# Four PSUM banks in turn for the mLSTM projections and gate tiles; modulation sums with two accumulators and a later row product

## The chip, the cores and the metric

The kernel runs on one core of a Trainium2 chip. The metric is the device time of one execution in microseconds (us), the median over several runs. TensorE is called PE in the profile (its weight loads PEld), VectorE DVE, ScalarE ACT, GpSimd POOL and SyncE SP; SP mostly issues transfers. PSUM is the memory that PE writes its results to. Here it is used as 8 banks of 128 partitions by 512 floats.

## The reference

One layer of a bidirectional sequence model, on 1024 latent tokens and 256 context tokens of width 1024, all in float32. Modulation is a matrix product of silu(c) with `w_mod`: its first 2048 columns shift and scale the tokens ahead of the mixing, the other 4096 gate and scale what comes later in the layer. Cut to what matters here:

```python
mod = silu(c) @ w_mod + b_mod                  # 6 pieces of 1024
sh1, sc1, g1, sh2, sc2, g2 = split(mod, 6)
p = u @ w_in + b_in                            # u: modulated tokens, latent and context
qk = silu(short_conv(concat([q_m, k_m]), conv_qk))        # 3 taps along the tokens
h_m = bidirectional(mlstm_scan, ...)           # 8 heads of width 128
h_g = bidirectional(gla_scan, ...)             # 4 heads, keys 128 wide, values 256
y_m = (head_norm(h_m) * sigmoid(o_m)) @ w_branch_mlstm
y_g = (head_norm(h_g) * silu(z_g)) @ w_branch_gla
mix = (sigmoid(gate_a) * y_m + sigmoid(gate_b) * y_g) @ w_out
h = layer_norm(ALPHA * x + g1 * mix)
out = layer_norm(ALPHA * h + g2 * conv_glu(h * (1 + sc2) + sh2))
```

## The kernel before

The program is written as straight Python over tiles. A framework's list scheduler then puts the instructions of each engine into a fixed order, in which the engine works them off; it also sets the waits between engines. A tile has a tag, and each tag has a number of buffers that its tiles take in turn: a new tile waits until the last reader of the tile that held its buffer before is done. The PSUM tags are `pj`, `pa`, `po` and `pt`, with two banks each.

Every product in float32 is made as three matmuls (`mm3`, L283 to L285): operands are split into a rounded high part and a rest (`whi` and `wlo` for weights, by ACT L252 and DVE L253), and high x high, high x low and low x high are added up in PSUM. The contraction of 1024 takes 8 such triples, so one group of 24 matmuls fills one bank. `proj(w, c, b, tag)` is one group: 128 output channels for block b of the tokens (b 0 and 1: 512 latent tokens each; b 2: the 256 context tokens), into a tile of the given tag, `pj` if none is given.

The stages that the change touches:

- *mLSTM heads* (about 500 to 1120 us). The loop over 8 heads issues the projections and convolution of the next head (`ml_proj_qk`: two groups for q, three for k), for even heads from 2 on the values of two heads (`ml_proj_v`), and the scan of the present head (`ml_scan`), then one or two gate tiles (`fill`, `gate_tile`: two groups each). A group of `ml_proj_qk` is read from PSUM by ACT (L732, the middle tap) and DVE (L727, the two outer taps, L737, the edge column that the next block needs; L743 and L745 correct the ends). A gate tile is read by ACT L537 and stored by an ACT transfer (L538) to `thb` or `tha`. `ml_scan` loads masks and gate rows by POOL transfers (L760, L761 `rr`, L764 `re`), of which ACT makes exponentials (L765, L769). Its PE steps: transposes of k (L777, `pt`), scores q x k (L786, two tiles of `pa`, read by DVE L788), state updates (L796, `pt`), outputs (L816 and L817, `po`). A head's end (L844 on PE, L845 on ACT) is issued one head later. The last GLA head, ahead of this stage, also leaves a `pa` tile that DVE L690 reads.
- *GLA branch with the modulation sums* (about 1195 to 1350 us). Eight output tiles j, each of two groups (24 matmuls), whose PSUM tag goes round `pj`, `pa`, `po` (`ytag`). For each tile SP loads `thb` (L953), ACT makes the tanh, DVE multiplies (L957) and SP stores `ya` (L958). Beside each tile one eighth of the 4096 late modulation columns is worked out: `mod_sum(j)` fills an accumulator with zeros (POOL L901), loads the bias into its first row (SP L903), loads `w_mod` in four pieces of 512 KB into two raw buffers in turn (u16 and u18, SP L906), and adds them up with eight DVE instructions (L908). `mod_row` sums over the 128 partitions by one PE instruction with a vector of ones (L913, into `pt`), which the profile counts as two matmuls; DVE copies the row back (L914) and SP stores it to `md_d` (L915).

The accumulators and raw buffers are tags with one buffer each, u16 to u19, which the gated stages before and after use for other things. The order of a loop body is where the scheduler starts from; it may move instructions past others.

Of the kernel before, what the change touches and what calls it, by code (L numbers as in the profile page):

```python
# [15 lines left out]
P = 128  # L16
# [20 lines left out]
def layer_kernel(ctx, tc, I, out, dbg=None):  # L37
# [39 lines left out]
    def ubt(i, shape, dt=F32):  # L77
        return ub.tile(shape, dt, tag=f"u{i}", name=nm(f"u{i}"))
# [35 lines left out]
    for l in range(7):  # L114
        h = 1 << l
# [207 lines left out]
    def proj(w, c, b, tag="pj"):  # L323
        p = pt(tag, [P, 512])
        mm3(p[:, 0:BW[b]], lambda k: w(k, c, P), u_blk(b))
        return p
# [202 lines left out]
            parts.append((hi, lo))  # L529
        return lambda k, c, n: tuple(t[:, k % 4, c:c + n] for t in parts[k // 4])  # L530

    def gate_tile(dst, off, cb0, j):
        w = wtile(w_in, off + j * P)
        for b in range(2):
            p = proj(w, 0, b)
            t = sc.tile([P, 512], F32, tag="gt", name=nm("gt"), bufs=2)
            A.activation(t[:], p[:], AF.Identity, scale=0.5, bias=cB(cb0 + j))  # L537
            A.dma_start(dst[j][:, b * 512:b * 512 + 512], t[:])  # L538
# [178 lines left out]
    def ml_proj_qk(h):  # L717
        w = wload([(w_in, O_QM + h * P, P, 0), (w_in, O_KM + h * P, P, P)])
        res = []
        for i in range(2):  # L720
            n = SEQ if i == 0 else L
            y = slot((0, 4)[h % 2] + i, [P, n])
            t0, t1, t2 = (cB(c_cv + 16 * j + 8 * i + h) for j in range(3))
            bs, b0, b2 = (cvb[:, j, 8 * i + h:8 * i + h + 1] for j in range(3))

            def tap(o, src, t):
                V.scalar_tensor_tensor(y[:, o:o + src.shape[1]], src, t, y[:, o:o + src.shape[1]],  # L727
                                       op0=ALU.mult, op1=ALU.add)
            for b in range(2 + i):
                m, o = BW[b], b * 512  # L730
                p = proj(w, i * P, b)
                A.activation(y[:, o:o + m], p[:, 0:m], AF.Identity, scale=t1, bias=bs)  # L732
                tap(o + 1, p[:, 0:m - 1], t0)
                tap(o, p[:, 1:m], t2)
                if b == 0:
                    ed = sc.tile([P, 1], F32, tag="ed", name=nm("ed"), bufs=2)
                    V.tensor_copy(ed[:], p[:, m - 1:m])  # L737
                if b == 1:
                    tap(o, ed[:], t0)
                    tap(o - 1, p[:, 0:1], t2)  # L740

                if b != 1:
                    V.tensor_tensor(y[:, o:o + 1], y[:, o:o + 1], b0, op=ALU.subtract)  # L743
                if b != 0:
                    V.tensor_tensor(y[:, o + m - 1:o + m], y[:, o + m - 1:o + m], b2, op=ALU.subtract)  # L745
            th = slot(15, [P, n])
            A.activation(th[:], y[:], AF.Tanh, scale=1.0 / QS if i == 0 else 1.0)
            V.scalar_tensor_tensor(y[:], th[:], 1.0, y[:], op0=ALU.add, op1=ALU.mult)
            res.append(y)
        return res  # L750
# [104 lines left out]

    gates = [(thb_d, O_GB, c_gb, j) for j in range(8)] + [(tha_d, O_GA, c_ga, j) for j in range(8)]

    def fill(n):
        for _ in range(n):
            gate_tile(*gates.pop(0))  # L860

    for h in range(GH):
        q, k = gla_qk(h) if h else (q0, k0)
# [13 lines left out]
    for h in range(MH):  # L877
        nxt = ml_proj_qk(h + 1) if h + 1 < MH else None
        if h and h % 2 == 0:
            v2 = ml_proj_v(h // 2)  # L880
        late()
        rest.append(ml_scan(h, *qk, v2[h % 2]))
        qk = nxt
        fill(2 if h < 2 or h > 5 else 1)
    late()
    while gates:
        fill(1)
# [9 lines left out]
        return tags[seq[0] % 3]  # L897

    def mod_sum(b):
        acc = ubt(19, [P, 512])  # L900
        G.memset(acc[:], 0.0)  # L901
        c0 = 2048 + b * 512
        SY.dma_start(acc[0:1, :], I["b_mod"][c0:c0 + 512].unsqueeze(0))  # L903
        for k2 in range(0, KD, 2):
            raw = ubt((16, 18)[k2 // 2 % 2], [P, 2, 512])
            SY.dma_start(raw[:], I["w_mod"][k2 * P:(k2 + 2) * P, c0:c0 + 512].rearrange("(k p) c -> p k c", p=P))  # L906
            for i in range(2):
                V.scalar_tensor_tensor(acc[:], raw[:, i, :], sC[:, k2 + i, 0:1], acc[:], op0=ALU.mult, op1=ALU.add)  # L908
        return acc

    def mod_row(b, acc):
        p = pt("pt", [P, 512])
        T.matmul(p[0:1, :], ones[:], acc[:], start=True, stop=True)  # L913
        V.tensor_copy(acc[0:1, :], p[0:1, :])  # L914
        SY.dma_start(md_d[b * 512:b * 512 + 512].unsqueeze(0), acc[0:1, :])  # L915

    def gated(off, cb0, src_d, silu):
        hi, lo = [], []
        for j2 in range(4):
            w = wload([(w_in, off + j2 * 256, 256, 0)])  # L920
            for e in range(2):
                j = 2 * j2 + e
                hi.append(slot(j, [P, SEQ], F32R))
                lo.append(slot(8 + j, [P, SEQ], F32R))
                hr = ubt(16 + j % 2, [P, SEQ])
                SY.dma_start(hr[:], src_d[j][:])
                ht = ubt(18, [P, SEQ])
                zz2 = ubt(19, [P, 2, 512]) if silu else None
                for b in range(2):
                    s_ = slice(b * 512, b * 512 + 512)  # L930
                    p = proj(w, e * P, b, ytag())
                    th = sc.tile([P, 512], F32, tag="gt", name=nm("gt"), bufs=2)
                    A.activation(th[:], p[:], AF.Tanh, scale=0.5, bias=cB(cb0 + j))
                    hs = hr[:, s_]
                    if silu:
                        zt = zz2[:, b, :]
                        A.activation(zt, p[:], AF.Identity, scale=0.5, bias=cB(cb0 + j))
                        V.tensor_tensor(hs, zt, hs, op=ALU.mult)
                    V.scalar_tensor_tensor(ht[:, s_], th[:], 1.0, hs, op0=ALU.add, op1=ALU.mult)
                    split(hi[j][:, s_], lo[j][:, s_], ht[:, s_])  # L940
        return hi, lo

    ya_d = [drt(f"ya{j}", [P, SEQ]) for j in range(8)]
    ghi_, glo_ = gated(O_ZG, c_zg, hg_d, True)
    for j2 in range(4):
        w = wload([(I["w_branch_gla"], j2 * 256, 256, 0)])
        for e in range(2):
            j = 2 * j2 + e
            acc = mod_sum(j)
            for b in range(2):  # L950
                s_ = slice(b * 512, b * 512 + 512)
                th = sc.tile([P, 512], F32, tag="gt", name=nm("gt"), bufs=2)
                SY.dma_start(th[:], thb_d[j][:, s_])  # L953
                A.activation(th[:], th[:], AF.Tanh)
                p = pt(ytag(), [P, 512])
                mm3(p[:], lambda k: w(k, e * P, P), lambda k: (ghi_[k][:, s_], glo_[k][:, s_]))
                V.scalar_tensor_tensor(th[:], th[:], 1.0, p[:], op0=ALU.add, op1=ALU.mult)  # L957
                SY.dma_start(ya_d[j][:, s_], th[:])  # L958
            mod_row(j, acc)

    rowF = ubt(19, [P, 3, P])
    cw = [I["ffn_conv_w"][a, b] for a in range(3) for b in range(3)]
# [305 lines left out]
```

## Time and profile before

| | |
|---|---|
| median of three runs | 2344.84 us (2343.28 to 2349.64) |
| profiled execution | 2350.07 us, its span 2348.3 us |
| mean granted PE clock | 0.988 |
| busy: PE, PEld, DVE, ACT, POOL | 96%, 84%, 58%, 31%, 13% |
| DMA over the span | 239.42 MB, mean 102 GB/s |
| chain that ended last | PE 29%, DVE 1%, others under 1% |

The page gives the busy time of each engine; a table by windows gives the same for any stretch of time with the granted clock; the list of waits says for each line of an engine which instruction it waited for last, for how long in all, how often, and the longest. In the timeline a row is a start, a duration, the engine, the line, the operation, output and input tiles; the bracket at its end is the idle time ahead of it and what ended it. Matmuls overlap, so their starts are to be compared, not their durations. A row that ends in x2 or more stands for several instructions in sequence.

### The profile page before, as it was taken

What the parts mean: (1) busy time and instruction counts of PE and PEld (TensorE: products, weight loads), DVE (VectorE), ACT (ScalarE), POOL (GpSimd) and SP (SyncE); (2) the same over time, 40 slices, a digit from 0 to 9 for tenths busy, and PEclk for the clock granted to TensorE, in tenths of its full rate; (3) what the DMA queues carried; (4) which work ended last, traced back from release to release, by engine and by line L of the source; (5) the groups of instructions that cost most, each with busy time, mean ns of one, the idle gap of its engine ahead of it and who ended that gap; (6) DMA issues with size and microseconds to landing.
All of it is one profiled execution on the core that took longest, in us unless ns stands there. A gap on an engine that the chain in (4) does not pass through costs nothing. (4 is left out here: it accounts for less than half of the span.)

```text
span 2348.3 us, 33481 instructions
## 1 busy us (share of the span) xinstructions
PE 2265.5 (96%) x13081; PEld 1965.0 (84%) x13081; DVE 1363.5 (58%) x2695; ACT 719.4 (31%) x1231; POOL 301.1 (13%) x254
## 2 busy tenths in 40 slices
PE   8989999998999999998999999999999999989998
PEld 4979898987889888897877788997888888889998
DVE  6484736475564645655345543577566556567457
ACT  3563323324332322313431143214333333311110
POOL 1010101111110111101210032101110000034300
PEclk9999999999999999999999999999999999999999
DMA  8222121203441333323357544512111122245511
GB/s 280 80 103 75 41 65 46 61 17 105 108 112 53 104 86 99 99 81 110 97 167 232 186 147 139 175 64 81 37 53 54 61 74 72 77 135 186 196 55 64
DMA packets 200848, 239.42 MB, mean 102 GB/s; under 512 B 16801, under 2 KB 155681, under 8 KB 200689
## 3 DMA queue, kind: packets, MB, share of 16 engines
q1 hardware_dynamic: 183521, 188.61, 25.8%
q0 software_dynamic: 8960, 31.63, 5.2%
q10 hardware_dynamic: 8208, 17.04, 2.0%
q8 instruction: 103, 1.69, 0.3%
q14 instruction: 56, 0.46, 0.1%
HBM read 183.42 MB, written 45.41 MB: 97 GB/s over the span
## 5 line engine op out<-in xcount | busy, mean ns | idle before, releaser
L252 ACT ACTIVATE whi<-raw 128x512 fp32r<-128x512 f32 x314 | 197.3, 630 | 516.1 <-PE pj L285 214.5
L283 PE MATMUL pj<-u,whi 128*128 128x512 f32 (+1 forms) x816 | 317.3, 389 | 20.3 <-DVE s L743 8.5
L253 DVE TENSOR_TENSOR wlo<-raw,whi 128x512 fp32r<-128x512 f32 x314 | 229.5, 735 | 157.5 <-ACT whi L252 153.4
L284 PE MATMUL pj<-u,whi 128*128 128x512 f32 (+1 forms) x816 | 314.3, 385 | 0.0
L285 PE MATMUL pj<-u,wlo 128*128 128x512 f32 (+1 forms) x816 | 313.8, 385 | 0.0
L283 PE MATMUL pj<-s,whi 128*128 128x512 f32 x784 | 305.6, 390 | 0.0
L285 PE MATMUL pj<-s,wlo 128*128 128x512 f32 x784 | 305.4, 390 | 0.0
L1120 DVE SCALAR_TENSOR_TENSOR acc<-g,colF,acc 128x945 f32<-128x945 f32 (+2 forms) x168 | 205.0, 1220 | 155.7 <-ACT acc L1111 153.6
L284 PE MATMUL pj<-s,whi 128*128 128x512 f32 x744 | 290.1, 390 | 2.3 <-POOL s L1075 2.3
L283 PE MATMUL pj<-whi,u 128*128 128x256 f32 x768 | 218.0, 284 | 0.0
L285 PE MATMUL pj<-whi,u 128*128 128x256 f32 x768 | 217.6, 283 | 0.0
L284 PE MATMUL pj<-wlo,u 128*128 128x256 f32 x768 | 217.6, 283 | 0.0
L283 PEld LDWEIGHTS pj<-u,whi 128*128 128x128 f32 x816 | 156.1, 191 | 51.2 <-ACT s L769 14.6
L285 PEld LDWEIGHTS pj<-u,wlo 128*128 128x128 f32 x816 | 156.0, 191 | 26.7
L284 PEld LDWEIGHTS pj<-u,whi 128*128 128x128 f32 x816 | 156.3, 192 | 25.9
L283 PEld LDWEIGHTS pj<-s,whi 128*128 128x128 f32 x784 | 147.2, 188 | 30.9
L285 PEld LDWEIGHTS pj<-s,wlo 128*128 128x128 f32 x784 | 147.2, 188 | 30.8
L284 PEld LDWEIGHTS pj<-s,whi 128*128 128x128 f32 x744 | 139.7, 188 | 33.0 <-POOL s L1075 3.6
L283 PEld LDWEIGHTS pj<-whi,u 128*128 128x128 f32 x768 | 147.4, 192 | 0.5
L284 PEld LDWEIGHTS pj<-wlo,u 128*128 128x128 f32 x768 | 147.4, 192 | 0.0
L285 PEld LDWEIGHTS pj<-whi,u 128*128 128x128 f32 x768 | 147.4, 192 | 0.0
L727 DVE SCALAR_TENSOR_TENSOR s<-pj,colB,s 128x511 f32<-128x511 f32 (+2 forms) x96 | 57.5, 613 | 92.2 <-ACT s L732 91.3
(486 smaller groups left out, 4479.8 us busy)
## 6 DMA issues: line engine op xcount, KB each, us to landing
u<-in_w_mod_dram SPq DMA_DIRECT2D x48, 512.0 KB
raw<-in_w_in_dram SPq DMA_DIRECT2D x96, 256.0 KB
raw<-in_w_up_dram SPq DMA_DIRECT2D x176, 128.0 KB
raw<-in_w_in_dram SPq DMA_DIRECT2D x96, 128.0 KB
raw<-in_w_down_dram SPq DMA_DIRECT2D x44, 256.0 KB
s<-rmask POOLq DMA_DIRECT2D x16, 512.0 KB, 5.2
s<-rr POOLq DMA_DIRECT2D x16, 512.0 KB, 7.9
qq<-re POOLq DMA_DIRECT2D x16, 512.0 KB, 6.5
```

The costliest lines, as they stand in the source:

```text
L252: A.activation(hi, src, AF.Copy)
L253: eng.tensor_tensor(lo, src, hi.bitcast(F32), op=ALU.subtract)
L283: T.matmul(p, lh, rh, start=k == 0, stop=False)
L284: T.matmul(p, lh, rl, start=False, stop=False)
L285: T.matmul(p, ll, rh, start=False, stop=k == nk - 1)
L727: V.scalar_tensor_tensor(y[:, o:o + src.shape[1]], src, t, y[:, o:o + src.shape[1]], op0=ALU.mult, op1=ALU.add)
L1120: V.scalar_tensor_tensor(av, g[:, r0 + dy:r1 + dy, c0 + dx:c1 + dx], convw(3 * ky + kx, f), av, op0=ALU.mult, op1=ALU.add)
```

## The change

Three things are changed. In `ml_proj_qk` the five groups of a head go to `pj` and `pa` in turn (q b0 pj, q b1 pa, k b0 pa, k b1 pj, k b2 pa) instead of all to `pj`. Gate tiles in the mLSTM loop put their second group into `pa`; in the GLA loop they stay with `pj`. And the modulation sums use u17 and u19 in turn as accumulator instead of u19 alone, and the row product of sum j is written behind tile j + 1 instead of behind tile j, the last one behind the loop.

```diff
--- before.py
+++ after.py
@@ -529,10 +529,10 @@
             parts.append((hi, lo))
         return lambda k, c, n: tuple(t[:, k % 4, c:c + n] for t in parts[k // 4])
 
-    def gate_tile(dst, off, cb0, j):
+    def gate_tile(dst, off, cb0, j, tags=("pj", "pj")):
         w = wtile(w_in, off + j * P)
         for b in range(2):
-            p = proj(w, 0, b)
+            p = proj(w, 0, b, tags[b])
             t = sc.tile([P, 512], F32, tag="gt", name=nm("gt"), bufs=2)
             A.activation(t[:], p[:], AF.Identity, scale=0.5, bias=cB(cb0 + j))
             A.dma_start(dst[j][:, b * 512:b * 512 + 512], t[:])
@@ -728,7 +728,7 @@
                                        op0=ALU.mult, op1=ALU.add)
             for b in range(2 + i):
                 m, o = BW[b], b * 512
-                p = proj(w, i * P, b)
+                p = proj(w, i * P, b, ("pj", "pa")[(i + b) % 2])
                 A.activation(y[:, o:o + m], p[:, 0:m], AF.Identity, scale=t1, bias=bs)
                 tap(o + 1, p[:, 0:m - 1], t0)
                 tap(o, p[:, 1:m], t2)
@@ -855,9 +855,9 @@
 
     gates = [(thb_d, O_GB, c_gb, j) for j in range(8)] + [(tha_d, O_GA, c_ga, j) for j in range(8)]
 
-    def fill(n):
+    def fill(n, tags=("pj", "pj")):
         for _ in range(n):
-            gate_tile(*gates.pop(0))
+            gate_tile(*gates.pop(0), tags)
 
     for h in range(GH):
         q, k = gla_qk(h) if h else (q0, k0)
@@ -881,7 +881,7 @@
         late()
         rest.append(ml_scan(h, *qk, v2[h % 2]))
         qk = nxt
-        fill(2 if h < 2 or h > 5 else 1)
+        fill(2 if h < 2 or h > 5 else 1, ("pj", "pa"))
     late()
     while gates:
         fill(1)
@@ -897,7 +897,7 @@
         return tags[seq[0] % 3]
 
     def mod_sum(b):
-        acc = ubt(19, [P, 512])
+        acc = ubt((17, 19)[b % 2], [P, 512])
         G.memset(acc[:], 0.0)
         c0 = 2048 + b * 512
         SY.dma_start(acc[0:1, :], I["b_mod"][c0:c0 + 512].unsqueeze(0))
@@ -942,11 +942,12 @@
 
     ya_d = [drt(f"ya{j}", [P, SEQ]) for j in range(8)]
     ghi_, glo_ = gated(O_ZG, c_zg, hg_d, True)
+    accs = {}
     for j2 in range(4):
         w = wload([(I["w_branch_gla"], j2 * 256, 256, 0)])
         for e in range(2):
             j = 2 * j2 + e
-            acc = mod_sum(j)
+            accs[j] = mod_sum(j)
             for b in range(2):
                 s_ = slice(b * 512, b * 512 + 512)
                 th = sc.tile([P, 512], F32, tag="gt", name=nm("gt"), bufs=2)
@@ -956,7 +957,9 @@
                 mm3(p[:], lambda k: w(k, e * P, P), lambda k: (ghi_[k][:, s_], glo_[k][:, s_]))
                 V.scalar_tensor_tensor(th[:], th[:], 1.0, p[:], op0=ALU.add, op1=ALU.mult)
                 SY.dma_start(ya_d[j][:, s_], th[:])
-            mod_row(j, acc)
+            if j:
+                mod_row(j - 1, accs[j - 1])
+    mod_row(7, accs[7])
 
     rowF = ubt(19, [P, 3, P])
     cw = [I["ffn_conv_w"][a, b] for a in range(3) for b in range(3)]
```

Line numbers up to L940 are the same in both programs; in the loop over the GLA tiles they are one higher behind the change (L953 is L954, L957 is L958, L958 is L959).

The first place is ACT's order in one head in the middle of the stage, around the reads of its q and k groups. In these rows `pj_993`, `_995`, `_998` and `_1000` are the groups q b0, q b1, k b0 and k b1, `s0` and `s1` hold q and k, `s6` and `s7` the masks, `qq` the gate rows. Before:

```order
L769 ACTIVATE s6_1008_7006<-s6_1008_7006,ta_4662 128x128 x7
L732 ACTIVATE s0_992_6828<-pj_993_6829,cvb_402,colB_389 128x512
L769 ACTIVATE s6_1008_7006<-s6_1008_7006,ta_4662 128x128
L769 ACTIVATE s7_1010_7021<-s7_1010_7021,ta_4662 128x128 x4
L765 ACTIVATE qq_1006_7004<-qq_1006_7004 128x1024
L769 ACTIVATE s7_1010_7021<-s7_1010_7021,ta_4662 128x128 x4
L732 ACTIVATE s0_992_6828<-pj_995_6860,cvb_402,colB_389 128x512
L747 ACTIVATE s15_996_6891<-s0_992_6828 128x1024
L732 ACTIVATE s1_997_6894<-pj_998_6895,cvb_402,colB_389 128x512
L732 ACTIVATE s1_997_6894<-pj_1000_6926,cvb_402,colB_389 128x512
```

Now:

```order
L769 ACTIVATE s6_1008_7006<-s6_1008_7006,ta_4662 128x128 x8
L732 ACTIVATE s0_992_6828<-pj_993_6829,cvb_402,colB_389 128x512
L769 ACTIVATE s7_1010_7021<-s7_1010_7021,ta_4662 128x128 x4
L765 ACTIVATE qq_1006_7004<-qq_1006_7004 128x1024
L769 ACTIVATE s7_1010_7021<-s7_1010_7021,ta_4662 128x128 x4
L732 ACTIVATE s0_992_6828<-pa_995_6860,cvb_402,colB_389 128x512
L747 ACTIVATE s15_996_6891<-s0_992_6828 128x1024
L732 ACTIVATE s1_997_6894<-pa_998_6895,cvb_402,colB_389 128x512
L732 ACTIVATE s1_997_6894<-pj_1000_6926,cvb_402,colB_389 128x512
```

The groups q b1 and k b0 have moved to `pa`; one exponential (L769) has gone ahead of the first L732, and else ACT's order is the same.

The second place is PE's order around the first row product (L913) of the branch stage. `pa_1511` is the first of the two groups of tile j = 1, `po_1512` in the new program the second, `pj_1532` the first group of tile 2, `u19_1495` and `u17_1495` the accumulator of sum 0. Before:

```order
L283 MATMUL pa_1511_10577<-s5_1444_10214,whi_1490_10462 128x512
L284 MATMUL pa_1511_10577<-s13_1445_10215,whi_1490_10462 128x512
L285 MATMUL pa_1511_10577<-s5_1444_10214,wlo_1491_10463 128x512
L913 MATMUL pt_1504_10551<-u19_1495_10472,ones_77 1x512
L283 MATMUL pa_1511_10577<-s6_1465_10308,whi_1493_10468 128x512
L284 MATMUL pa_1511_10577<-s14_1466_10309,whi_1493_10468 128x512
```

Now:

```order
L285 MATMUL po_1512_10603<-s6_1465_10308,wlo_1494_10469 128x512
L283 MATMUL po_1512_10603<-s7_1474_10378,whi_1493_10468 128x512
L284 MATMUL po_1512_10603<-s15_1475_10379,whi_1493_10468 128x512
L285 MATMUL po_1512_10603<-s7_1474_10378,wlo_1494_10469 128x512
L913 MATMUL pt_1513_10630<-u17_1495_10472,ones_77 1x512
L283 MATMUL pj_1532_10680<-s0_1377_9818,whi_1515_10636 128x512
L284 MATMUL pj_1532_10680<-kk_1378_9819,whi_1515_10636 128x512
```

Before, the first L913 stands behind 18 of the 24 matmuls of a group of tile 1, with 67 to 77 rows from each L913 to the next and the last three behind the start of the next gated stage. Now it stands behind the last matmul of tile 1, and the next six follow at the end of a tile each (49 rows apart); the eighth comes 27 rows into the next gated stage.

The third place is SP's order around the store of the first row (L915) and the bias load (L903) of a later sum. Before:

```order
L906 DMA u18_1507_10562<-in_w_mod_dram 128x2x512
L953 DMA gt_1512_10604<-thb1_867 128x512
L915 DMA md_d_9785<-u19_1495_10472 1x512
L958 DMA ya1_9787<-gt_1510_10574 128x512
L263 DMA raw_1553_10840<-in_w_branch_gla_dram 128x2x256
L903 DMA u19_1505_10555<-in_b_mod_dram 1x512
L953 DMA gt_1532_10681<-thb2_868 128x512
```

Now:

```order
L959 DMA ya1_9787<-gt_1511_10600 128x512
L915 DMA md_d_9785<-u17_1495_10472 1x512
L906 DMA u16_1527_10661<-in_w_mod_dram 128x2x512
L954 DMA gt_1533_10707<-thb2_868 128x512
L903 DMA u17_1526_10658<-in_b_mod_dram 1x512
L906 DMA u18_1528_10665<-in_w_mod_dram 128x2x512
L959 DMA ya2_9788<-gt_1531_10677 128x512
```

Before, the bias load for sum 1 follows the store of row 0, since both use u19. Now the bias loads of sums 0 and 1 stand together ahead of these rows, and behind the store of row 0 comes the bias load of sum 2, with the first piece of `w_mod` for that sum ahead of it.

## The prediction

> **What bounds the kernel now.** I first read the page's busy shares, then a table by stage, then PE's waits in the two stages that the change touches, and last the timeline around single waits.
>
> ```profile
> PE 2265.5 (96%) x13081; PEld 1965.0 (84%) x13081; DVE 1363.5 (58%) x2695; ACT 719.4 (31%) x1231; POOL 301.1 (13%) x254
> ```
>
> PE is busy 96% of a span of 2348.3 us, so only PE's idle time and its slow-clock time can be had: every other engine counts only where it makes PE wait. The profiled execution took 2350.07 us, 5.2 above the median of 2344.84. By stage (stretch and length, then busy time and instructions of PE, PEld, DVE, ACT, POOL, then granted clock, DMA share, GB/s):
>
> ```profile
> 480.00:640.00 160.00, 150.34 (x855) 129.56 (x856) 100.88 (x221) 56.67 (x113) 23.54 (x26) 0.97 0.30 81
> 640.00:840.00 200.00, 194.53 (x1191) 172.09 (x1191) 118.06 (x363) 56.30 (x112) 23.52 (x24) 0.99 0.34 93
> 840.00:1100.00 260.00, 245.38 (x1574) 220.56 (x1573) 141.60 (x436) 76.40 (x162) 33.85 (x29) 0.97 0.34 93
> 1195.00:1365.00 170.00, 161.24 (x664) 123.38 (x663) 89.64 (x129) 38.99 (x64) 15.04 (x17) 0.98 0.64 201
> ```
>
> The mLSTM heads (480 to 1100) leave PE idle for 30 us of 620, the GLA branch with the modulation sums (1195 to 1365) for 9 of 170. PE's waits, from 480 to 1120 and then from 1195 to 1365, with POOL's there (total us, times, longest):
>
> ```profile
> PE pj L283 <- DVE s L743: 8.5, 4, 2.9
> PE pt L777 <- ACT s L845: 6.1, 1, 6.1
> PE pj L283 <- DVE s L727: 5.5, 3, 2.7
> PE pj L283 <- ACT gt L537: 5.2, 2, 2.7
> ```
> ```profile
> PE pt L913 <- DVE u L908: 5.4, 5, 2.1
> PE pt L913 <- issue: 3.3, 2, 1.7
> ```
> ```profile
> POOL u L901 <- DMA md_d<-u: 128.4, 7, 20.0
> ```
>
> The three rows `pj L283` are 19.2 us in nine waits: a projection wants a pj bank that its evacuation has not left. The L777 row waits for an operand, which no bank cures. The L913 rows, 8.7 us in seven waits, are the row product waiting for its sum. One `pj` wait close up, PE first, then ACT, then DVE:
>
> ```profile
> 787.17 0.39 PE L285 MATMUL pj<-u,wlo 128*128 128x512 f32 x1
> 790.42 0.77 PE L283 MATMUL pj<-u,whi 128*128 128x512 f32 x1 [2.86 <-DVE s L743]
> 793.12 0.47 PE L283 MATMUL pj<-u,whi 128*128 128x512 f32 x1
> 793.43 0.39 PE L284 MATMUL pj<-u,whi 128*128 128x512 f32 x1
> 793.65 0.39 PE L285 MATMUL pj<-u,wlo 128*128 128x512 f32 x1
> 785.74 2.16 ACT L769 ACTIVATE s<-s,ta 128x128 f32<-128x128 f32 x7 [2.31 <-DMA s<-rr]
> 787.80 0.76 ACT L732 ACTIVATE s<-pj,cvb,colB 128x512 f32<-128x512 f32 x1
> 788.67 1.53 DVE L727 SCALAR_TENSOR_TENSOR s<-pj,colB,s 128x511 f32<-128x511 f32 x2 [7.72 <-ACT s L732]
> 790.24 0.16 DVE L743 TENSOR_TENSOR s<-s,cvb 128x1 f32<-128x1 f32 x1
> ```
>
> At full clock these matmuls start 0.22 to 0.23 us apart (793.43, 793.65), so a group of 24 is 5.45 us. The last matmul before the wait (787.17) closes the second group, so the first ended at about 781.9. Its evacuation (L732, two L727, the edge columns) ends at 790.4, 8.5 us after the group, because ACT works in order and stood first behind the gate exponentials L769, which had waited for a transfer of `rr`. With two banks the third group needs the bank 5.45 us after the first ended, so 3 us are lost. After the wait the clock is low: from 790.42 to 793.12 there are six steps in 2.70 us, 1.33 more than at full clock, and the next step is 0.31; that is 1.4 us more for such a wait. I count such a slow stretch, by this spacing, after four of the seven waits outside head 0 (636, 790, 930, 991).
>
> By the Trainium skill, page "TensorE: Matmul & The Clock Gate", section "What's actually happening", the clock falls only after an idle window of about 3.4 us. By that rule waits of 2 to 3 us would cost no slow clock, and the gain below would be about 14 us instead of 23.5. The measured spacing after 2.86 us decides against it here.
>
> **The change part by part.** It adds no matmul, no transfer and no evacuation.
>
> *Banks in turn, heads 1 to 7.* Groups go q b0 pj, q b1 pa, k b0 pa, k b1 pj, k b2 pa, and a gate tile takes one of each. A bank now comes back after two groups or more, 10.9 us, against 8.5 us for the late evacuation above: the wait is gone with 2.4 us to spare, and the cover for all of it is ACT's lateness staying under 10.9. Removed: 19.2 less the two waits of head 0 (2.49 and 0.92, rows below) is 15.8 us in seven waits. Each gap exceeds its recorded wait by 0.16 (787.17 to 790.42 is 3.25, less a step of 0.23, against 2.86), 1.1 in all. Four slow stretches are 5.6. Together 22.5; at least 15.8 if only recorded waits return.
>
> *pa is shared with the score matmuls L786.* Their first group holds a pa bank until DVE's L788; the gate tile's second half wants it some 9 us later in the order. If L788 is as late as the 8.5 above, that is no wait. Their second group comes 2.9 us after k b2 in heads 0, 1, 3 and 5, in the bank that k b2 used. That evacuation is seen here, where k b2's last matmul stands just ahead of L844:
>
> ```profile
> 805.62 1.03 PE L844 MATMUL pt<-ident,s 128*128 128x128 f32 x8
> 808.23 0.47 DVE L727 SCALAR_TENSOR_TENSOR s<-pj,colB,s 128x255 f32<-128x255 f32 x1
> ```
>
> It ends at 808.7, some 3 us behind: waits of 0 to 0.8, and I take 0.4, four times, minus 1.6. In heads 2, 4 and 6 a v projection lies between.
>
> *Head 0.* The last GLA head's output holds the second pa bank until L690, behind these groups, so three groups of head 0 share one pa bank.
>
> ```profile
> 547.96 0.77 PE L283 MATMUL pj<-u,whi 128*128 128x512 f32 x1 [2.49 <-DVE s L743]
> 565.14 0.47 PE L283 MATMUL pj<-u,whi 128*128 128x512 f32 x1 [0.92 <-DVE s L727]
> 551.95 1.66 DVE L727 SCALAR_TENSOR_TENSOR s<-pj,colB,s 128x511 f32<-128x511 f32 x3 [4.00 <-ACT s L732]
> 553.65 0.15 DVE L745 TENSOR_TENSOR s<-s,cvb 128x1 f32<-128x1 f32 x1
> ```
>
> The old waits cost 2.49 + 0.92 + 1.4 of slow clock, 4.8. Now k b0 follows q b1 into the same bank. PE arrives at 545.47 (547.96 less 2.49); 16 matmuls of k b1 stand ahead in the new order (3.6 us), so it stops at 549.1 and waits until q b1 is out, 553.7: 4.6 plus 1.4 is 6.0. Net minus 1.2 (plus 1 if ACT gets q b1 sooner, minus 4 if k b2 then waits as well). Heads: 22.5 - 1.6 - 1.2 = 19.7 us, between 14 and 24.
>
> *Two accumulators and the row one tile later.* Today's sums follow one chain; one link of it on PE, SP, POOL and SP:
>
> ```profile
> 1239.49 1.02 PE L913 MATMUL pt<-u,ones 128*1 128x512 f32 x2 [1.60 <-issue]
> 1241.25 0.25 SPq L915 DMA_DIRECT2D md_d<-u  x1
> 1243.48 0.53 POOL L901 MEMSET u<- 128x512 f32 x1 [20.02 <-DMA md_d<-u]
> 1244.03 0.25 SPq L903 DMA_DIRECT2D u<-in_b_mod_dram  x1
> ```
>
> From the row product to the next bias load 4.5 us pass, and the load must land before a sum starts; with two accumulators this runs beside the other sum. What can be saved: 8.7 recorded, 0.16 for each of seven, and two slow stretches of 1.4, one in each window with a clock of 0.91:
>
> ```profile
> 1215.00:1235.00 20.00, 18.27 (x71) 13.71 (x70) 10.79 (x16) 4.31 (x7) 0.53 (x1) 0.91 0.71 227
> 1255.00:1275.00 20.00, 19.56 (x83) 14.84 (x82) 10.40 (x15) 3.03 (x5) 0.53 (x1) 1.00 0.77 244
> 1295.00:1315.00 20.00, 18.08 (x70) 14.01 (x71) 10.11 (x15) 4.37 (x7) 0.53 (x1) 0.91 0.65 198
> ```
>
> In all 12.6 us. What is late next is the sum's own pace T per tile: both raw buffers are loaded twice for each sum, 512 KB a load. SP's issues of three pairs of consecutive rounds:
>
> ```profile
> 1230.83 1.95 SPq L906 DMA_DIRECT2D u<-in_w_mod_dram  x2
> 1236.77 3.03 SPq L906 DMA_DIRECT2D u<-in_w_mod_dram  x2
> 1268.33 1.96 SPq L906 DMA_DIRECT2D u<-in_w_mod_dram  x2
> 1273.91 0.38 SPq L906 DMA_DIRECT2D u<-in_w_mod_dram  x1
> 1287.59 1.95 SPq L906 DMA_DIRECT2D u<-in_w_mod_dram  x2
> 1295.32 1.96 SPq L906 DMA_DIRECT2D u<-in_w_mod_dram  x2
> ```
>
> Rounds of 5.94, 5.58 and 7.73, mean 6.42, so T is 12.8 us (11.2 to 15.5). I take the mean, since the rounds to come meet the same other transfers. What PE allows: its first row product stands 29 rows later in the new order (5508 against 5479), so near 1223.1, where today's, without its wait, would stand at about 1216.5; the eighth stands 321 rows behind it, 314 matmuls of 0.227 and seven row products of 1.02, so at 1301.5 if PE never waits. The first sum is ready at about 1219.3, a microsecond later than today's (a second fill and bias load go ahead of it), the eighth at 1219.3 + 7T = 1308.9. PE loses 7.4 there, plus 1.4 of slow clock: 8.8, and the net is 12.6 - 8.8 = plus 3.8. With T at 11.2 it is plus 12.6, with 15.5 minus 15. Behind a late load on SP's queue stand the th loads and ya stores; their banks are three tags of two, 32 us deep.
>
> Sum: 19.7 + 3.8 = 23.5 us, from 2350.07 to 2326.6 in this execution; against the median, 2321.
>
> **The rivals.**
> *A. The sums fall behind* (T from 14 to 16.2). For it: the round of 7.73, and DMA engines 64% busy in that stage, which a denser program pushes up. Against it: two of three rounds are under 6. At T = 15 the eighth sum is at 1324.3, PE loses 22.8 + 1.4 against 12.6, 11.6 net, so the gain is 8 us: 2337.
> *B, the other side: the second accumulator does not speed the sums.* If they keep today's spacing of 18.9 us (128.4 / 7 between memsets, and the memset's 0.53) while PE wants rows every 11.9, the eighth sum is at 1351.6: a loss of 50.1 + 1.4 - 12.6 = 38.9, so 19 us slower after the banks' gain: 2364. The whole gain is gone from T = 16.2, and a loss shows from 17.2. Against it: 4.5 us and the bias landing of each 18.9 are the chain that goes.
> *C. The evacuation itself is the limit*: ACT's lateness (8.5 here) passes 10.9 when PE runs ahead, so waits only move to pa, as in head 0. Then the banks give 5, and with 4 from the sums 2336. Against it: DVE is 58% busy and ACT 31%, and the transfers that hold ACT are started after PE's own steps.
> *D. The clock.* If going from bank to bank made PE stumble at each group, 40 q and k groups and 24 gate halves at 1.4 us would cost 90 us: about 2411. Against it: the GLA branch already changes banks among pj, pa and po with each group, and its clock is 1.00 in the window from 1255. The Trainium skill, same page, section "A second HAM failure mode: psum-queue depth-cycling", reports such a case for N=512 matmuls; that row does not agree.
> *E. The sums keep up* (T under 11.9): hardly a wait at all, 30 to 36 us gained, 2308 to 2315.
>
> **How the numbers follow.** Chances: forecast 0.60 (banks 18 to 23, T 11.9 to 14: 2312 to 2331), A 0.13, B 0.05, C 0.10, D 0.02, E 0.10. A measurement of this kernel tells 0.3%, 7 us, from no change: same is 2338 to 2352. Faster: 0.60, 0.08 of A, 0.05 of C and all of E, 0.83. Same: 0.05 of A, 0.04 of C, 0.09. Slower: B, D and 0.01 of C, 0.08. The range 2308 to 2337 leaves out B, D, half of C and half of A.
>
> **What would show it.** Right: from 480 to 1080 the `L283` waits on L743, L727 and L537 are gone but for one of 4 to 6 us in head 0; small waits stand at L786; the L777 wait of 6 us stays. In the branch stage the memsets hardly wait for md_d, rounds of w_mod come every 6 to 6.5 us, and PE waits about 7 us at the last two L913. Wrong: `pa` rows waiting on L727 in many heads (C), L913 waits over all tiles and above 20 us (A, B), or a clock under 0.98 without waits (D).

## The result, and the profile after

| | before | after |
|---|---|---|
| median, first comparison | 2344.06 us (2342.15 to 2349.64) | 2324.14 us (2320.30 to 2327.47) |
| ratio | | 0.9911 (0.9887 to 0.9934) |
| median, second comparison | 2345.23 us (2339.88 to 2349.63) | 2323.13 us (2320.71 to 2323.88) |
| ratio | | 0.9906 (0.9891 to 0.9920) |
| profiled execution, its span | 2350.07, 2348.3 us | 2320.30, 2318.5 us |

The change is worth about 20 to 22 us. The pair of profiles lies 29.8 us apart, since that of before is one of the longest runs of its kernel and that of after the shortest of its own; stage times below are therefore compared over several traces. The page's busy row and the table by stage, with the columns as before:

```profile
PE 2254.1 (97%) x13081; PEld 1958.9 (84%) x13081; DVE 1362.8 (59%) x2695; ACT 719.3 (31%) x1231; POOL 300.4 (13%) x254
```
```profile
480.00:640.00 160.00, 152.83 (x887) 133.10 (x886) 101.22 (x225) 56.84 (x114) 24.67 (x27) 0.98 0.30 79
640.00:840.00 200.00, 199.82 (x1223) 177.16 (x1222) 121.70 (x371) 64.60 (x133) 27.99 (x27) 1.00 0.37 101
840.00:1100.00 260.00, 254.19 (x1635) 229.30 (x1634) 148.05 (x465) 74.86 (x154) 29.54 (x27) 0.99 0.34 96
1180.00:1350.00 170.00, 166.17 (x694) 127.59 (x693) 92.16 (x133) 41.98 (x69) 19.78 (x20) 0.99 0.66 213
```

From 640 to 840 PE is now busy for all but 0.2 us, with the clock at 1.00; before it lacked 5.5. All other engines have the same work. PE's waits in the two stages (480 to 1105, then 1085 to 1460; rows under 1 us left out):

```profile
PE pt L777 <- ACT s L845: 5.7, 1, 5.7
PE pt L501 <- DVE ta L502: 3.2, 1, 3.2
PE pa L283 <- DVE s L727: 3.1, 1, 3.1
```
```profile
PE pj L283 <- ACT whi L252: 3.8, 1, 3.8
```

Of the nine bank waits of the q, k and gate groups (19.2 us) one is left, in head 0; a tenth, of 1.1 us on DVE L713 behind a value group of head 0, which the prediction did not count, is gone too. All waits at L913 are gone in this trace, and one new wait for weights stands at the start of the next gated stage. The same place as in the prediction, a head in the middle, rows of PE, ACT and DVE:

```profile
776.16 0.39 PE L285 MATMUL pj<-u,wlo 128*128 128x512 f32 x1
776.39 0.39 PE L283 MATMUL pa<-u,whi 128*128 128x512 f32 x1
781.83 0.39 PE L283 MATMUL pa<-u,whi 128*128 128x512 f32 x1
787.27 0.39 PE L283 MATMUL pj<-u,whi 128*128 128x512 f32 x1
780.36 2.45 ACT L769 ACTIVATE s<-s,ta 128x128 f32<-128x128 f32 x8 [2.73 <-DMA s<-rr]
782.71 0.75 ACT L732 ACTIVATE s<-pj,cvb,colB 128x512 f32<-128x512 f32 x1
783.58 1.53 DVE L727 SCALAR_TENSOR_TENSOR s<-pj,colB,s 128x511 f32<-128x511 f32 x2 [8.30 <-ACT s L732]
785.15 0.16 DVE L743 TENSOR_TENSOR s<-s,cvb 128x1 f32<-128x1 f32 x1
```

ACT still waits for `rr`, and the first group (its last matmul at 776.16) is read out by 785.3, 8.7 us after its end. Nothing has become faster here; but q b1 (776.39), k b0 (781.83) and k b1 (787.27) start 5.44 us apart without a gap; before, the third group waited 2.86 us for the bank of the first, and now q b1 and k b0 go to `pa` and k b1 to the other `pj` bank. The sums, by POOL's fills of the accumulators, PE's row products, the start of the gated stage on PE and the last adds on DVE:

```profile
1208.06 0.53 POOL L901 MEMSET u<- 128x512 f32 x1 [24.81 <-DVE u L908]
1221.11 0.53 POOL L901 MEMSET u<- 128x512 f32 x1 [12.52 <-DMA md_d<-u]
1234.09 0.53 POOL L901 MEMSET u<- 128x512 f32 x1 [12.45 <-DVE u L908]
```
```profile
L913 PE MATMUL pt<-u,ones x16: 590/591/592, 1200.4 to 1287.4; 128*1 128x512 f32 x16
```
```profile
1237.31 1.02 PE L913 MATMUL pt<-u,ones 128*1 128x512 f32 x2
1282.03 0.79 PE L283 MATMUL pj<-u,whi 128*128 128x512 f32 x1 [3.83 <-ACT whi L252]
1282.62 0.63 PE L284 MATMUL pj<-u,whi 128*128 128x512 f32 x1
1284.91 1.54 DVE L908 SCALAR_TENSOR_TENSOR u<-u,sC,u 128x512 f32<-128x512 f32 x2 [0.74 <-DMA u<-in_w_mod_dram]
```

The fills come 13 us apart instead of 18.9. The first sum ends at 1196.2 and the eighth at 1286.45 (1284.91 + 1.54), so one each 12.9 us. PE puts a row product every 12.3 us. It comes 4.2 us after the first sum (1200.4), and as the sums fall behind by 0.6 each, it comes 0.7 after the seventh. It stands half a microsecond behind the eighth only because the wait for weights and the slow steps after it, 5.6 us together, lie ahead of that row: without them it would have been there at 1281.4, 5.1 us too early. These are the loads of `thb` and of the weights on SP, and what ACT made of them:

```profile
1275.90 0.42 SPq L954 DMA_DIRECT2D gt<-thb  x1
1276.37 0.47 SPq L263 DMA_DIRECT2D raw<-in_w_in_dram  x1
1280.60 0.63 ACT L955 ACTIVATE gt<-gt 128x512 f32<-128x512 f32 x1 [5.82 <-DMA gt<-thb]
1281.34 0.63 ACT L252 ACTIVATE whi<-raw 128x512 fp32r<-128x512 f32 x1
```

ACT stood behind the `thb` load for 5.82 us and split the weights (L252) right after; the trace does not show whether the weights had landed before that.

Stage times over several traces: "heads" from the last L672 to the last L844, "branch" from there to the first transpose of `rowF` (L1022, or L1025 behind the longer loop), all taken from the starts on PE; "rest" is what follows to the end of the span. The stretch ahead of the heads, 500 to 504 us in these traces, is left out.

| kernel | heads | branch | rest |
|---|---|---|---|
| before | 613.1 | 374.9 | 859.4 |
| after | 587.3 | 368.2 | 859.5 |
| after, second trace | 588.8 | 370.4 | 861.8 |
| banks alone | 588.4 | 376.4 | 860.5 |
| sums alone | 607.4 | 371.9 | 859.8 |
| two accumulators alone | 608.1 | 376.3 | 861.5 |
| q and k groups alone | 587.1 | 373.7 | 862.5 |
| q and k all on pa | 604.8 | 372.5 | 861.3 |

Heads with the old banks (before, sums alone, two accumulators alone): mean 609.5; with the new ones (the two traces of after, banks alone): 588.2. That is 21.3 us. The branch with the old sums (before, banks alone, the two q/k kernels): mean 374.4; with the new ones (after twice, sums alone): 370.2, that is 4.2 us. The rest is the same within about 3 us, so that a difference of that size in one stage of one trace says little.

### The profile page after: what moved, and what is told of

Its sections match the earlier page's. It is cut to its first block, busy times and chain, and to the rows that moved or that the text cites. A ratio compares the mean times of both kernels' runs of the same rounds, so it can differ in the third digit from the quotient of the medians.

```text
span 2318.5 us, 33477 instructions
## 1 busy us (share of the span) xinstructions
PE 2254.1 (97%) x13081; PEld 1958.9 (84%) x13081; DVE 1362.8 (59%) x2695; ACT 719.3 (31%) x1231; POOL 300.4 (13%) x254
## 3 DMA queue, kind: packets, MB, share of 16 engines
q1 hardware_dynamic: 183521, 188.61, 25.8%
## 5 line engine op out<-in xcount | busy, mean ns | idle before, releaser
L252 ACT ACTIVATE whi<-raw 128x512 fp32r<-128x512 f32 x314 | 196.7, 630 | 467.9 <-PE pj L285 212.0
L283 PE MATMUL pj<-u,whi 128*128 128x512 f32 (+1 forms) x528 | 207.5, 393 | 3.9 <-ACT whi L252 3.8
L285 PE MATMUL pj<-u,wlo 128*128 128x512 f32 (+1 forms) x528 | 206.2, 390 | 0.0
L284 PE MATMUL pj<-u,whi 128*128 128x512 f32 (+1 forms) x528 | 206.0, 390 | 0.0
L283 PE MATMUL pa<-u,whi 128*128 128x512 f32 (+1 forms) x376 | 141.2, 376 | 3.1 <-DVE s L727 3.1
L284 PE MATMUL pa<-u,whi 128*128 128x512 f32 (+1 forms) x376 | 141.1, 375 | 0.0
L285 PE MATMUL pa<-u,wlo 128*128 128x512 f32 (+1 forms) x376 | 140.2, 373 | 0.0
L283 PEld LDWEIGHTS pj<-u,whi 128*128 128x128 f32 x528 | 100.4, 190 | 23.2 <-ACT whi L252 4.3
```

The source lines that it names most:

```text
L252: A.activation(hi, src, AF.Copy)
L283: T.matmul(p, lh, rh, start=k == 0, stop=False)
L284: T.matmul(p, lh, rl, start=False, stop=False)
L285: T.matmul(p, ll, rh, start=False, stop=k == nk - 1)
```

## The experiments

**Both halves, and the whole again.** The whole change, repeated:

> The whole change once more, to size it: one profile of each kernel shows 29.8 us between them, the medians 19.9. My sum gives 23.5 us, a ratio of 0.990. If the profile pair is the better measure, 0.987; if the medians are, 0.9915. In the trace no pj wait of over 1 us between 500 and 1080 but two in head 0 (about 3 us each), and no wait at L913.

0.9906 (0.9891 to 0.9920), 22.1 us between the medians; no pj wait in the heads, waits of 2.7 and 3.2 in head 0, none at L913, and 4.9 us for the weights of the next gated stage. The medians were the better measure, not the pair of profiles. The banks alone (the lines that pass `tags` on are left out):

```diff
-                p = proj(w, i * P, b)
+                p = proj(w, i * P, b, ("pj", "pa")[(i + b) % 2])
-            p = proj(w, 0, b)
+            p = proj(w, 0, b, tags[b])        # gate tiles of the mLSTM loop: pj, pa
```

> Only the banks in turn (q/k groups and gate tiles), sums as before. Theory: the seven pj waits outside head 0 and their slow clock go, 20 to 23 us, ratio 0.990 to 0.9915, and the L913 waits stay at 8 to 10 us. Rival (the bank waits were only covering waits on ACT's late evacuation that come back elsewhere): under 8 us, ratio above 0.9965, with pa waits on L727 or L537 in several heads.

0.9927 (0.9915 to 0.9939), 17.5 us between the medians. That is a little under the theory's range, and more than double the rival's 8. PE's waits in the heads are those of the whole change, and no other `pa` wait stands there; those of the branch are as before:

```profile
PE pt L913 <- DVE u L908: 7.3, 5, 2.8
PE pt L913 <- issue: 3.0, 2, 1.7
```

The sums alone (the lines that keep the accumulators in `accs` are left out):

```diff
-        acc = ubt(19, [P, 512])
+        acc = ubt((17, 19)[b % 2], [P, 512])
-            mod_row(j, acc)
+            if j:
+                mod_row(j - 1, accs[j - 1])
+    mod_row(7, accs[7])
```

> Only the sums (two accumulators, row product a tile later), banks as before. Theory: a sum each 12.9 us against a PE tile of 12.3 us, so the L913 waits of 8.7 us and two slow stretches go but for one wait of about 4 us at the start of the next gated stage: 6 to 9 us, ratio 0.996 to 0.9975; the pj waits stay at 19 us. Rival (sums bound by the two raw buffers as before): 0 to 3 us.

0.9987 (0.9976 to 0.9998), 3.7 us between the medians: nearer to the rival's 0 to 3 than to the 6 to 9 that I expected. The pj waits are there (16.9 us, and 1.2 at L713, where the trace of before has 19.2 and 1.1), and in the branch stand

```profile
PE pt L913 <- DVE u L908: 3.9, 4, 1.5
PE pj L283 <- ACT whi L252: 3.2, 1, 3.2
```

So 7.1 us of waits stand where the trace of before has 8.7: most of what L913 gave back was taken by the weights' wait. The sums' pace here is 13.6 us from the first end (1213.5) to the eighth (1308.6), well under the 18.7 of before, so the raw buffers did not hold them at the old pace as the rival had it; but it is 0.7 above the 12.9 that the theory took, and the lead of 4.9 us that PE leaves the first sum is used up by the fourth. The whole change is near the same edge: with the same sums, the L913 waits are nothing in both of its traces and 1.6 to 2.2 us in four of the five kernels below that keep whole sums and the later row, at a pace of 12.9 to 13.4 us.

**Two accumulators alone**, with the row product behind its own tile (only the first changed line of the diff above):

> Only the two accumulators; the row product is written behind its own tile as before, which puts the first L913 30 rows (7 us) and the last 14 rows (3 us) ahead of its place in the whole change. Theory: the pace of the sums alone sets it, 12.9 us each, so the eighth sum comes some 8 us after PE wants it: L913 waits of 7 to 10 us in total, spread over the tiles, gain 1 to 4 us, ratio 0.9985 to 0.9995. Rival (the second accumulator is all that counts, the later row nothing): as the sums alone, 6 to 9 us.

1.0010 (1.0001 to 1.0019): no gain, against both. The L913 waits are 10.3 us,

```profile
PE pt L913 <- DVE u L908: 7.3, 5, 3.2
PE pt L913 <- issue: 3.0, 1, 3.0
```

just above the 7 to 10 expected and no less than before, although the eighth sum now ends at 1310.7 instead of 1349.5 (34 us earlier if counted from the stage's start, the last L844). The scheduler has also moved the row products ahead on PE, the last by 164 matmuls of PE's order: it has spent in advance what the faster sums gain. With the row a tile later PE comes 4.9 us (the sums alone) or 4.2 us (the whole change) after the first sum instead of waiting for it, and the slower sums live on that lead.

**Q and k groups alone**, gate tiles left on pj, sums as before (only the first line of the first diff):

> The q and k groups in turn on pj and pa, gate tiles all on pj, sums as before. Theory (a bank is late when it comes back after one group, 5.45 us, and its evacuation ends 7 to 9 us after the group): the waits on L743, L727 and L737 go, and those on L537 (5.2 us, two) go too, since k's groups no longer stand in the pj banks ahead of the gate tiles' second use: 17 to 20 us, ratio 0.9915 to 0.993, as the banks with the gates. Rival (each kind of tile needs its own four banks): the two waits on L537 stay, about 7 us with their slow clock, ratio 0.995.

0.9913 (0.9900 to 0.9927), 19.0 us: the gain of the banks is there without the gate tiles. No wait on L537 is left in the heads:

```profile
PE pt L777 <- ACT s L845: 5.9, 1, 5.9
PE pt L501 <- DVE ta L502: 3.2, 1, 3.2
PE pa L283 <- DVE s L727: 1.5, 1, 1.5
PE pt L501 <- ACT whi L252: 0.5, 1, 0.5
PE pa L786 <- DVE s L727: 0.4, 1, 0.4
```

**All q and k groups on pa**, the control for the theory of the distance:

```diff
-                p = proj(w, i * P, b)
+                p = proj(w, i * P, b, "pa")
```

> All q and k groups on pa, gate tiles on pj, sums as before: as many banks in the stage as with the change, but q and k have two in turn. Theory (what counts is the number of groups until a bank comes back): the waits of 2.5 to 3 us return at `pa <- DVE s L743` and `L727`, 12 to 16 us with head 0, and only the two waits on L537 go: gain 4 to 8 us, ratio 0.9965 to 0.998. Rival (q and k were held up by gate and value tiles in the same two banks, and four banks for the stage are enough however they are dealt): 15 to 20 us, ratio 0.992 to 0.9935.

1.0009 (0.9998 to 1.0019): no gain. The waits are back under the other name, 15.2 us, within the 12 to 16 of the theory:

```profile
PE pa L283 <- DVE s L743: 9.8, 5, 3.0
PE pa L283 <- DVE s L727: 4.1, 3, 1.7
PE pa L283 <- ACT s L769: 1.3, 1, 1.3
```

The waits on L537 went, as expected, but the gain of 4 to 8 us did not come. Its heads are 4.7 us shorter than the mean of the old ones in the one trace, which with 2341.07 us was the shortest of its ten runs (median 2348.80). This trace has one slow stretch at a projection outside head 0, where that of before has four, and its mean granted clock is 0.991 against 0.987 to 0.990 in the nine others; more slow stretches there would fit, but no trace shows them. For the rival it is decisive: the stage has the same four banks here, and what counts is how many groups pass until a bank comes back (the releasers L743 and L727 are the evacuation of q and k, not the score tiles that share `pa`).

**Gate tiles left on pj, with the sums:** the change less its gates' part.

> The whole change with the gate tiles left in pj. Theory (the q and k groups in turn remove the gate tiles' waits too, so the gates' own turn is worth nothing): within 2 us of the whole change, ratio to before 0.9895 to 0.9915, and no wait on L537. Rival (the stage times of the q/k version, 587.1 us for the heads against 588.4 with the gates, show that gate tiles in pa cost something at L786): 2 to 4 us below the whole change, ratio 0.989 or less.

0.9889 (0.9872 to 0.9906), 27.8 us between the medians, with the before of this comparison at 2347.84 against 2344.1 to 2345.4 in the others. No wait on L537 came back. Its own median, 2320.03, is 3.1 below the whole change, but the intervals overlap (0.9891 to 0.9920), and its trace, of the longest of its five runs (2325.86), shows no shorter stage (heads 591.0, branch 369.7). By the ratio it lies on the rival's side, but no term of the trace carries that; the runs can't tell the gates' part from nothing.

**Head 0 on po instead of pa:**

```diff
-                p = proj(w, i * P, b, ("pj", "pa")[(i + b) % 2])
+                p = proj(w, i * P, b, ("pj", "pa" if h else "po")[(i + b) % 2])
```

> The whole change, but head 0 takes po instead of pa, whose banks are not held by the last GLA head's late tile. Theory (the remaining wait at k b0 of head 0, 2.5 to 3.1 us in three traces, is a bank held by that tile): it goes with its slow clock, 3 to 4.5 us below the whole change, ratio to before 0.9885 to 0.9895. Rival (ACT's waits for the mask and gate-row transfers in head 0 are what PE waits for): the wait moves to the next use of a bank or to L777 of head 0, 0 to 1 us, ratio 0.9905.

0.9921 (0.9908 to 0.9933), 17.8 us: no better than the whole change. The wait at k b0 has gone, so it was that bank; but the time has not:

```profile
PE pt L692 <- DVE hn L690: 2.5, 1, 2.5
```

PE now waits nearly as long at the transposes of the last GLA head, whose operand DVE L690 makes behind the late taps. The rival is nearer in time and named the wrong place; for its cause speaks that in this trace ACT waits 8.52 us for a mask and 1.64 us for `rr` (L769) among the reads of these groups.

**Half of each sum:** only two of the four `w_mod` pieces are loaded and added.

> The whole change with only the first two of the four w_mod pieces loaded and added per sum: half of each sum is left out. Theory (after the change the wait of 3 to 5 us at the start of the next gated stage, `pj L283 <- ACT whi L252`, comes from SP and the DMA engines being filled with w_mod and the sums only just keep up): sums of 6 to 7 us, no wait at L913, and the whi wait shrinks under 1.5 us: 3 to 6 us below the whole change, ratio 0.988 to 0.9895. Rival (the weights of the gated stage are late because of the order on SP, behind ya stores that follow PE): the wait stays at 3 to 5 us and the time within 2 us of the whole change.

0.9901 (0.9886 to 0.9917), 0.4 us from the whole change between the medians. The wait for weights is gone, but a wait at L913 of almost the same length has come:

```profile
PE pt L913 <- DVE u L908: 4.3, 1, 4.3
```

Two things moved with the shorter sums. The scheduler put the weights' loads for the next gated stage ahead on SP (the third is issued at 1248.81, in the whole change at 1276.37), so this run does not tell whether the filled DMA engines or the order on SP made them late. And it put the eighth row product directly behind the seventh; the eighth sum, whose accumulator comes free only after the sixth row product, is ready at 1278.35 for a PE that is there 4 us before. So neither theory holds for the time: one wait has taken the place of the other, as in the whole change the eighth sum (1286.45) ends 4.4 us after the wait for weights does (1282.03).

**The transposes at a head's end, and half of the gate tables, in po instead of pt:** the first edit alone, the second alone, and both.

```diff
-                p = pt("pt", [P, 4, P])          # L844, finish of ml_scan
+                p = pt("po", [P, 4, P])
-                p = pt("pt", [P, 8, 64])         # L501
+                p = pt("pt" if j0 == 0 else "po", [P, 8, 64])
```

> The whole change, with the two transposed tiles at a head's end (L844) in po instead of pt. The wait of 5.3 to 6.1 us at L777 in the last head is there in every trace; its releaser L845 reads pt. Theory (this too is a bank that comes back while ACT is late, and no wait for an operand): it goes, 4 to 7 us with its slow clock, ratio to before 0.988 to 0.989. Rival (ACT's late exponentials are needed next, at L816, and nothing else is left to do in the last head): the same time is lost at L816 or L796, 0 to 1.5 us gained.

> The whole change, with the second of each two gate-table tiles (L501) in po instead of pt. Theory (the wait `pt L501 <- DVE ta L502`, 3.2 us now and 1.8 before the change, is a pt bank that waits for its copy): it goes, and head 0's other wait of 2.5 to 3 us at k b0 becomes longer by as much, since that bank's time does not depend on PE: 0 to 2 us gained in all. Rival (each wait is separate): 3 to 4.5 us, ratio 0.989.

> Both moves to po together, on the whole change. Theory: the sum of the two single ones within 2 us, so 4 to 8 us below the whole change, ratio to before 0.987 to 0.989. Rival (ACT's lateness after the transfers of rr is what ends last in heads 0 and 7): within 1.5 us of the whole change, 0.990 to 0.991.

0.9917 (0.9899 to 0.9935), 0.9924 (0.9909 to 0.9940) and 0.9923 (0.9909 to 0.9938): none is better than the whole change; the medians lie 1.3, 4.5 and 2.6 us above it, so all three theories missed. The rivals of the first and third are nearer and missed by a little over 1 us; the first named the wrong place (L816 or L796). The releasers changed, the waits hardly did. The first three rows are of the first kernel, the other two of the second:

```profile
PE pt L777 <- DVE kk L780: 6.0, 1, 6.0
1059.00 1.29 DVE L253 TENSOR_TENSOR wlo<-raw,whi 128x512 fp32r<-128x512 f32 x2 [13.03 <-ACT whi L252]
1060.21 3.31 DVE L780 TENSOR_TENSOR kk<-pt,twk 128x256 f32<-128x256 f32 x6
```
```profile
PE pa L283 <- ACT qq L765: 4.0, 1, 4.0
PE pt L501 <- ACT s L474: 2.9, 1, 2.9
```

In the last head L777 now waits for DVE, which evacuates its own `pt` tile (L780) behind a split of weights that stood 13 us for ACT: ACT is late again, by another way. That in heads 0 and 7 there is too little other work for PE while ACT stands behind the transfers, so that another bank only moves the place at which PE runs out, fits all three runs but is a reading of them. Of the kernels tried none is clearly better than the change.

## Why the prediction was right

Right: 2321 us was forecast, 2324.14 measured, in the range; 23.5 us of gain against 19.9 and 22.1 in two comparisons. The mechanism of the banks held; that the total came so near is in part luck. Between the trace that the sum was worked out from and that of after the heads are 25.8 us shorter, not 19.7, and the branch 6.7, not 3.8. But that trace was a long one (2350.07 us), and the sum was taken off the median of 2344.84, so that the two errors cancelled.

- *Banks, 22.5 in heads 1 to 7.* The mechanism is shown from both sides: the evacuation is still 8.7 us late and no wait follows, and on two banks of another name the waits return. All seven waits and their slow clock went (no slow stretch is left at a projection outside head 0). The whole term for the heads, 19.7, stands against 21.3 between the stage means, and 17.5 between the medians of the banks alone. My base was one execution, and in the heads it was 5 us longer than two others with the same banks (613.1 against 607.4 and 608.1). I took four slow stretches, 5.6 us, from it as if they were fixed; those two traces have two and three, after much the same waits.
- *Gate tiles.* I put the 5.2 us behind L537 down to two tiles that take one of each tag. They needed no tags: with q and k spread, the gate tiles' pj banks come back late enough.
- *L786, minus 1.6.* Mis-sized: in the trace of after no wait stands there (in three other kernels 0.4, 0.9 and 1.4).
- *Head 0, minus 1.2.* The wait at k b0 came, 3.1 us and not 4.6, and without a slow clock (in the second trace 2.7, with one); but L501 waits 3.2 now against 1.8. PE that came earlier to the tables waits there: I had not priced this.
- *L777.* I read this row as a wait for an operand. L777 and L845 share the tag pt, so it is a bank too. The conclusion that it stays held (5.7 us), for another reason: with L844 in another bank the same time is lost at the next tile of L777.
- *Sums, plus 3.8.* The stage means give 4.2, the sums alone 3.7. The pace T was right: 12.9 and 13.1 in the two traces of the whole change against 12.8. Two other terms were off and cancelled in part, which is luck. PE's tile is 12.3 us and not 11.9, since the matmuls of this stage start 0.232 us apart (below); so PE would have stood 5.1 us, not 7.4, before the eighth sum. And the wait came at another row: weights of the gated stage, whose load stands on SP between the loads of `w_mod`, were split 3.8 us late, followed by a slow stretch. My account had the th loads behind a late load, and ACT did stand behind one (5.82 us); it had not the weights that come after it on ACT.
- *The later row.* I took it and the second accumulator as one edit. Alone the second accumulator gave nothing, with the rows moved ahead by the scheduler; only the two edits together gave the 3.7.

Rival A's pace (14 us and more) was not reached in any trace with two accumulators and whole sums (12.9 to 13.7); B's (18.9) and C's growing lateness are refuted by the rows above; D by the clock of 1.00 from 640 to 840, where banks change at every group. E's sign, no wait at L913, came, but by a longer tile and a wait elsewhere.

## What to carry to other kernels

A wait for a PSUM bank is priced by two times: how late the evacuation ends after its group (here 8.5 to 8.7 us), and how long the groups last until the bank comes back (5.45 before, 10.9 after). If the second exceeds the first the wait goes, with the evacuation as slow as ever; two more banks that left q and k the same number of groups gained nothing here. A slow stretch after a wait is no fixed price: count it over several executions. And when a chain is shortened under a list scheduler, look at where the consumer now stands: it may have been moved ahead by as much as was gained.

## What the runs showed of the hardware that was not expected

Whether a wait is followed by a slow clock follows neither from its length nor from its place. After a wait of 2.86 us (before, at 790.42) six steps took 2.70 us instead of 1.36. In the same trace 2.71 us (852.30) were followed by no slow step, and 1.88 us (990.46), three steps later, by seven of 0.43 us. The wait at k b0 of head 0 went both ways in two traces of the same kernel: in the second trace of after 2.67 us were followed by seven steps of 0.43 us, in the first the matmuls came at full pace after 3.12:

```profile
556.23 0.47 PE L283 MATMUL pa<-u,whi 128*128 128x512 f32 x1 [3.12 <-DVE s L727]
556.54 0.39 PE L284 MATMUL pa<-u,whi 128*128 128x512 f32 x1
556.77 0.39 PE L285 MATMUL pa<-u,wlo 128*128 128x512 f32 x1
556.99 0.39 PE L283 MATMUL pa<-u,whi 128*128 128x512 f32 x1
```

The Trainium skill ("TensorE: Matmul & The Clock Gate", "What's actually happening") counts idle time in free-running windows of about 3.4 us. Whether the place of a wait against such a window decides, no run here shows.

The branch's matmuls, of the same shape as those of the projections and at clock 1.00, start 0.23 to 0.24 us apart:

```profile
1226.75 0.40 PE L283 MATMUL pa<-s,whi 128*128 128x512 f32 x1
1226.99 0.39 PE L284 MATMUL pa<-kk,whi 128*128 128x512 f32 x1
1227.22 0.39 PE L285 MATMUL pa<-s,wlo 128*128 128x512 f32 x1
1227.45 0.39 PE L283 MATMUL pa<-s,whi 128*128 128x512 f32 x1
```

The mean is 0.232 us over the branch against 0.227 in the projections. The cause stays open.
